# A decoder block on one core: the SSD's output product by pairs of blocks in seven products, with h parked in memory meanwhile

## The chip, the core and the metric

The kernel runs on one core of a Trainium2 chip. A core has TensorE (PE, matrix products into the PSUM banks; its weight loads are listed as PEld), VectorE (DVE), ScalarE (ACT), GpSimd (POOL) and SyncE (SP). SP's queue issues nearly all DMAs here, one after the other in the order of its program. Metric: device time of one execution in microseconds (us), lower is better.

## What is computed

One decoder block on a sequence of 1024 tokens of width 1024, all in float32. The part that matters here:

```python
h = rms_norm(x, pre_norm1_w) * (1.0 + sc1) + sh1
proj = h @ w_in
z, xbc, dt_raw, q, k, v, gates = split(proj)
y_ssd = ssd_branch(z, xbc, dt_raw, ...)             # 1024 x 1024
y_att = diff_attention_branch(q, k, v, ...)         # partial rope on q and k
gate_ssd, gate_att = split(sigmoid(gates))
merged = gate_ssd * (y_ssd @ w_ssd_o) + gate_att * (y_att @ w_attn_o)
mix = merged @ w_out
...                                                 # norms, adaLN gates, conv-FFN
```

The change is about `gate_ssd * (y_ssd @ w_ssd_o)`, which stands between the SSD scan and the attention.

## The kernel before

Every float32 operand of a matmul is split into a high and a low part (type fp32r: ACT copies the high part, DVE subtracts it to get the low one), and a product is three matmuls: high by high, high by low, low by high (`mm3`). A 128 x 512 result over 1024 rows is 8 k-tiles x 3 = 24 matmuls (`block_half`). Activations lie transposed: `hT[k][half]` holds rows 128k of h for 512 tokens, high and low.

Memory on the chip is handed out by `Slots`: 43 slots of 512 KB, first freed, first given again. A tile that gets a freed slot waits for the last use of the tile before it. `hT` holds 16 of the slots from the start of the kernel to the end of the attention.

The order of the work: h; seven-product loops for gates, two q/k blocks and the convolved channels (`pairs`, see below); z; the SSD scan in 16 steps with v's product as filler; then the stage of the change; then attention, with the remaining q/k blocks and the attention's gates as filler (`dense_stream`, `blocks`); its output product; `w_out`; the FFN.

Inside a `with tc.manual_schedule(...)` section the instructions of the engines named there (PE, DVE, ACT and SP for the stages before the attention) run in the order in which the code issues them. Between sections the scheduler may put the first instructions of the next one earlier.

The stage of the change, before:

* Four q/k blocks, `seq` = q0, k0, q1, k1, each for both halves of the tokens. Between the halves TensorE turns the scan's output y (`turn_y`, four transposes per 128 channels and half): ACT scales it into the high part, DVE makes the low part, in `yT[k][half]`. y comes token-wise from memory in four tiles `yr`; `load_y(0)` is issued during the scan, `load_y(1)` after the last turn of the first half.
* `rope` of a finished q/k block: ACT copies it from PSUM, DVE shuffles, POOL and DVE multiply by the tables, DVE adds, `split` makes high and low, and `store_qk` writes them with 16 DMAs of 64 KB. In the loop, `load_y(1)` is called ahead of that `store_qk`:

```python
                if n == 1 and half == 0:
                    load_y(1)
                if half == 0 and old is not None:
                    store_qk(*old[:2], hi, lo)
```

* Eight blocks of `w_ssd_o`, 48 matmuls each; DVE multiplies by (1 + gate) from `gth` (memory `gsd`) and SP writes `msd`. `load_qk(0)` and `load_qk(1)`, which fetch q and k of the first head pair for the attention, are issued at blocks 3 and 4.

The seven-product loop, which exists for gates, q2/k2 and channels: two output blocks (rows of a weight pair) by two halves of tokens, over two halves of the 1024 rows, are a 2 x 2 by 2 x 2 block product. `order` lists the seven products with the bank X, Y or Z that they add to; `HX` holds the right operands (b11, b21, b22 and the sums t1 to t4), `x_sum` and `x_split` make the left ones from the weights, `x_load` fetches these, `x_ahead(m, p)` prepares product p of pair m three products ahead, `x_mms` issues its 12 matmuls. Between the products ACT copies bank X or Y (`ev_`) and DVE adds.

The first attention items: 14 fills of three matmuls each, then `scores(0)`, which needs both tiles that `load_qk` fetched.

Of the kernel before, what the change touches and what calls it, by code (L numbers as in the profile page):

```python
# [62 lines left out]
def kernel(ctx: ExitStack, tc: tile.TileContext, a: dict, out: bass.AP, dbg=None):  # L63
# [306 lines left out]


# [44 lines left out]
    def x_load():  # L416
# [4 lines left out]
        src = {"gs": ("w_gate", "w_gate"), "xbc": ("w_xbc", "w_xbc"), "qk": ("w_q", "w_k")}[kind]["fv".index(n)]  # L421
# [109 lines left out]
    with tc.manual_schedule(engines={EN.PE, EN.DVE, EN.Activation, EN.SP}):  # L531
# [100 lines left out]
        for m, (kind, *_) in enumerate(pairs):  # L632
# [10 lines left out]
            for p in range(7):  # L643
# [161 lines left out]
    def ada_row(r):  # L805
# [7 lines left out]
        if r in (0, 3):  # L813
            ps, row = ps_wb(f"adar{r}"), sm2[:KD, 896 : 896 + P]
            T.transpose(ps[:KD, :P], c_, ident)
            V.tensor_copy(row, ps[:KD, :P])
            SP.dma_start(rowd[r].rearrange("o (k p) -> (o k) p", p=P), row)

    last_pair = len(pairs) - 1
    with tc.manual_schedule(engines={EN.PE, EN.DVE, EN.Activation, EN.SP}):  # L820
        for t_, (c0, wdt) in enumerate(thirds):
# [4 lines left out]
            for i in range(8):  # L826
# [257 lines left out]
    seq = [("w_q", 0), ("w_k", 0), ("w_q", 1), ("w_k", 1)] + [("w_ssd_o", j) for j in range(8)]  # L1084
# [12 lines left out]
    n_skip = 0  # L1097

    def sum_dn(u):
        nonlocal n_skip  # L1100
        if u in (7, 8) and n_skip < 4:
            n_skip += 1
        else:
            next(sums_dn, None)

    with tc.manual_schedule(engines={EN.PE, EN.DVE, EN.Activation, EN.SP}):
# [19 lines left out]
        for u in range(16):  # L1126
# [5 lines left out]
            sum_dn(u)  # L1132
# [3 lines left out]
            sum_dn(u)  # L1136
# [6 lines left out]
            sum_dn(u)  # L1143
# [3 lines left out]
            sum_dn(u)  # L1147
# [26 lines left out]
    yT = [[None] * 2 for _ in range(KD)]  # L1174

    n_turn = 0


    def turn_y(k, half):
        yT[k][half] = new_hl(f"yT{k}_{half}")  # L1180
        nonlocal n_turn
        ps = (ps_wa, ps_wb, ps_wa, ps_wc)[n_turn % 4](f"ytr{k}_{half}")
# [4 lines left out]
        A.activation(yT[k][half][:, 0, :], ps, AF.Copy, scale=nw)  # L1187
        V.scalar_tensor_tensor(yT[k][half][:, 1, :], ps, nw, yT[k][half][:, 0, :].bitcast(F32), op0=ALU.mult, op1=ALU.subtract)
# [4 lines left out]
    perm = [(i + 8) % 16 + 16 * (i // 16) for i in range(32)]  # L1193
    def split_seq(n):
# [6 lines left out]
    def rope(kind, b, ps):  # L1201
        A.activation(qf, ps.rearrange("p h t -> p (h t)"), AF.Copy, scale=qscale[kind])
        V.stream_shuffle(sw, qf, perm)
        G.tensor_tensor(qf, qf, ropc, op=ALU.mult)
        V.tensor_tensor(sw, sw, rops, op=ALU.mult)
        V.tensor_tensor(qf, qf, sw, op=ALU.add)
        split(hi, lo, qf)

    turns = [((0, 1), (2, 3, 4)), ((5, 6, 7), ()), ((0, 1), (2, 3)), ((4, 5), (6, 7))]
    with tc.manual_schedule(engines={EN.PE, EN.DVE, EN.Activation, EN.SP}):  # L1210
        split_seq(0)
        old = None
        for n in range(4):
            fetch_seq(n + 2)
            ps = ps_mm(f"{seq[n][0]}p{seq[n][1]}")
            for half in range(2):
                block_half(ps[:, half, :], seq_w[n], hT, half)
                if half == 0:
                    if old is not None:
                        rope(*old)  # L1220
                    split_seq(n + 1)
                for k in turns[n][half]:
                    turn_y(k, n // 2)
                if n == 1 and half == 0:
                    load_y(1)
                if half == 0 and old is not None:
                    store_qk(*old[:2], hi, lo)
            old = (*seq[n], ps)
        SL.put(*yr)


        gths = [SL.get(f"gth{i}") for i in range(2)]
# [1100 lines left out]
```

## Time and profile before

| | us |
|---|---|
| median of 3 runs | 1862.75 (1860.8 to 1863.04) |
| the profiled execution | 1863.45 |
| its span (first to last instruction) | 1861.5 |
| PE busy | 1827.3 |
| DVE busy | 1290.8 |
| ACT busy | 888.4 |
| POOL busy | 141.6 |

Rows of the profile read: line, engine, operation, output <- input, shapes, count, then busy time or start and length. "idle before <- X" names what ended the wait ahead of an instruction. SPq rows are DMA issues on SP's queue; their length is the time of the issue, not of the transfer. Stretches are given in us from the start of the span.

### The profile page before, as it was taken

The page shows a single profiled execution, that of the slowest core. Times are in us where ns is not written, and L with a number is a line of the kernel's source. Part 1 is how long each engine was busy: PE and PEld are TensorE (multiplying, and loading weights), DVE is VectorE, ACT ScalarE, POOL GpSimd, SP SyncE. Part 2 cuts the span into 40 slices and gives each one's busy share as a digit, 9 for nine tenths or more (in the row PEclk, how much of TensorE's full clock was granted, in tenths as well). Part 3 has the DMA queues.
Part 4 walks back from the last instruction along what each step waited for, and adds up shares of the span by engine and source line. Part 5 has one row for each costly group of instructions (what it writes and reads, how often), then busy time and mean ns, then how long its engine had stood idle before and what let it go on. Part 6 is the DMA issues. An engine that isn't in the chain of part 4 may idle for free.

```text
span 1861.5 us, 24406 instructions
## 1 busy us (share of the span) xinstructions
PE 1827.3 (98%) x8974; PEld 1528.6 (82%) x8974; DVE 1290.8 (69%) x1980; ACT 888.4 (48%) x1720; POOL 141.6 (8%) x128
## 2 busy tenths in 40 slices
PE   6999999999999999999999999999999999999998
PEld 4888889987888888888887888888888888888887
DVE  6777857688755247777767464487898888876545
ACT  6644543455533136565656322564545455455532
POOL 0000000155521000000000000000000000000001
PEclk9999999999999999999999999999999999999999
DMA  8365356587747746656643655123333323378754
GB/s 329 134 215 181 102 190 226 182 313 278 261 128 189 237 136 180 169 162 182 171 130 120 234 195 203 45 91 106 101 116 109 111 86 107 108 229 297 252 159 164
DMA packets 130217, 322.57 MB, mean 173 GB/s; under 512 B 14881, under 2 KB 38833, under 8 KB 130098
## 3 DMA queue, kind: packets, MB, share of 16 engines
q1 hardware_dynamic: 129138, 317.86, 52.6%
q0 software_dynamic: 960, 3.15, 0.5%
q8 instruction: 71, 1.16, 0.3%
q14 instruction: 48, 0.39, 0.1%
HBM read 225.79 MB, written 95.17 MB: 172 GB/s over the span
## 4 chain that ended last, share of the span: by engine, by line
PE 82%; DVE 8%; ACT 4%; DMA 4%; issue 2%; SPq 1%; POOL 0%; DVEq 0%; POOLq 0%; ACTq 0%
PE upx L1741 4%; PE upx L1742 4%; PE upx L1740 4%; PE o L1435 3%; PE upy L1741 2%; PE upy L1740 2%; PE upy L1742 2%; PE dx L2104 2%; PE dx L2105 2%; PE dx L2103 2%; PE dy L2105 2%; PE dy L2103 2%; PE dy L2104 2%; PE at L1422 2%; PE sc L1377 2%
## 5 line engine op out<-in xcount | busy, mean ns | idle before, releaser
L1740 PE MATMUL upx<-t,wu_t 128*128 128x512 f32 x264 | 103.1, 391 | 0.5 <-DVE cv L2168 0.4
L1741 PE MATMUL upx<-t,wu_t 128*128 128x512 f32 x264 | 102.8, 390 | 0.2 <-DVE t L1858 0.2
L1742 PE MATMUL upx<-t,wu_t 128*128 128x512 f32 x264 | 102.7, 389 | 0.0
L1714 ACT ACTIVATE wu_t<-sab 128x512 fp32r<-128x512 f32 x57 | 34.1, 627 | 128.4 <-DVE sab L1731 128.4
L1423 ACT COPY aT<-at 128x512 f32<-128x512 f32 (+2 forms) x96 | 46.1, 480 | 96.0 <-PE at L1422 96.0
L1435 PEld LDWEIGHTS o<-vt,aT 128*128 128x128 f32 x576 | 75.3, 191 | 9.2 <-ACT aT L1423 4.6
L95 DVE TENSOR_TENSOR g_lo<-gst,g_hi 128x1024 fp32r<-128x1024 f32 (+1 forms) x42 | 47.5, 1134 | 50.0 <-ACT g_hi L94 50.0
L1435 PE MATMUL o<-vt,aT 128*128 128x128 f32 x576 | 80.9, 276 | 0.4
L94 ACT ACTIVATE g_hi<-gst 128x1024 fp32r<-128x1024 f32 (+1 forms) x42 | 41.3, 987 | 64.7 <-DMA gst<-gld_s 36.3
L1396 DVE TENSOR_REDUCE nmx<-sc 128x1 f32<-128x640 f32 (+3 forms) x64 | 65.6, 1024 | 2.2
L1376 PE MATMUL sc<-kst,qst 128*128 128x512 f32 (+2 forms) x192 | 63.8, 340 | 0.0
L1377 PE MATMUL sc<-klo,qst 128*128 128x512 f32 (+2 forms) x192 | 63.3, 346 | 0.0
L1758 DVE SCALAR_TENSOR_TENSOR ug<-cg,vec,ug 128x1023 f32<-128x1023 f32 (+1 forms) x44 | 56.3, 1280 | 6.1 <-ACT ug L1757 5.3
L1740 PEld LDWEIGHTS upx<-t,wu_t 128*128 128x128 f32 x264 | 49.6, 188 | 11.6 <-DVE cv L2168 1.3
L1741 PEld LDWEIGHTS upx<-t,wu_t 128*128 128x128 f32 x264 | 49.6, 188 | 10.7 <-DVE t L1858 0.5
L1742 PEld LDWEIGHTS upx<-t,wu_t 128*128 128x128 f32 x264 | 49.6, 188 | 10.2
L1718 DVE TENSOR_TENSOR wu_t<-sab,wu_t 128x512 fp32r<-128x512 f32 x57 | 39.3, 690 | 26.6 <-ACT wu_t L1714 26.6
L1758 DVE SCALAR_TENSOR_TENSOR uv<-cv,vec,uv 128x1023 f32<-128x1023 f32 (+1 forms) x44 | 56.2, 1277 | 0.9 <-ACT uv L1757 0.9
L1414 DVE SCALAR_TENSOR_TENSOR p<-p,coef,p 128x128 f32<-128x128 f32 (+3 forms) x64 | 52.4, 818 | 2.3
L1412 DVE RECIPROCAL rsm<-ssum 128x2 f32<-128x2 f32 x64 | 10.6, 165 | 62.4 <-ACT p L1409 35.2
L2224 POOL TENSOR_TENSOR rsf<-rsf,nhalf 128x1 f32<-128x1 f32 x8 | 5.3, 656 | 624.3 <-DVE rsf L2223 624.3
L2104 PE MATMUL dx<-wdt_lo,g_hi 128*128 128x512 f32 x132 | 51.5, 390 | 0.0
(537 smaller groups left out, 5921.7 us busy)
## 6 DMA issues: line engine op xcount, KB each, us to landing
adas<-in_w_ada SPq DMA_DIRECT2D x32, 512.0 KB, 5.0
wdr<-in_w_down SPq DMA_DIRECT2D x22, 512.0 KB, 5.6
wtd<-wds SPq DMA_DIRECT2D x22, 512.0 KB, 4.0
wuf<-in_w_up SPq DMA_DIRECT2D x22, 512.0 KB, 3.5
gld_s<-gsum SPq DMA_DIRECT2D x22, 512.0 KB, 2.8
gst<-gld_s SPq DMA_DIRECT2D x20, 512.0 KB, 4.6
wdt_raw<-wtd SPq DMA_DIRECT2D x20, 512.0 KB, 5.0
wuv<-in_w_up SPq DMA_DIRECT2D x19, 512.0 KB, 3.5
```

The lines of the kernel that those rows point to most:

```text
L1376: T.matmul(sc[:, n0:n1], qs_[s][:, tsl], ks_[s][:, n0:n1], start=True, stop=False)
L1377: T.matmul(sc[:, n0:n1], qs_[s][:, tsl], kl[s][:, n0:n1], start=False, stop=True)
L1396: V.reduce_max(nmx[:, bq, s : s + 1], sc[:, :L], axis=AX.X, negate=True)
L1414: V.scalar_tensor_tensor(pr[0][:, :L], pr[1][:, :L], coef[:, bq : bq + 1], pr[0][:, :L], op0=ALU.mult, op1=ALU.add)
L1435: T.matmul(po_of[j, grp][:, qi, :], at[:, k, :], vt[j % 2][:, kt, :], start=(kt == 0), stop=(kt == i))
L1740: T.matmul(out_, wh, xh_, start=(k == 0 and first), stop=False, skip_group_check=not first)
L1741: T.matmul(out_, wh, xl_, start=False, stop=False, skip_group_check=not first)
L1742: T.matmul(out_, wl, xh_, start=False, stop=(k == end), skip_group_check=not first)
L1758: V.scalar_tensor_tensor(u[:, d:], c_[:, : S - d], fw[:, 2 - d : 3 - d], u[:, d:], op0=ALU.mult, op1=ALU.add)
L2103: T.matmul(o, gh[:, kk, tsl], wh, start=(k == 0 and not more), stop=False, skip_group_check=more)
L2104: T.matmul(o, gh[:, kk, tsl], wl, start=False, stop=False, skip_group_check=more)
L2105: T.matmul(o, gl[:, kk, tsl], wh, start=False, stop=(k == KF - 1), skip_group_check=more)
```

## The change

The eight blocks of `w_ssd_o` become four pairs of the seven-product loop: 4 x 7 x 12 = 336 matmuls in place of 384. That needs the sums of y's quarters as operands, in float32 and split: `y11, y21, y12, y22`, and `HX` of b11, b21, t2, t1, t3, b22, t4 (28 slots). For these h leaves the chip:

* 12 of the 16 tiles of `hT` are written to memory (`hd`) in the earlier loop of pairs, at pairs 4 to 6; the other four are there already (`h12d`). `h_back` reloads all 16, four at product 5 of the third pair and four at each of the products 0 to 2 of the last.
* The q/k blocks run as (0,0) (0,1) (1,0) (1,1) (2,0) (3,0) (2,1) (3,1), in (block, half), so that the first halves of h are done early. The turns of y's second half come at (1,1), (2,0) and (3,0).
* `rope` becomes a generator of four steps, the last of which calls `store_qk`. For blocks 0 and 1 it runs at once (`rope_now`); for 2 and 3 a step after each product of the new loop.
* `load_qk(0)` and `load_qk(1)` move to products 5 and 6 of the last pair; `fetch(0)` and `fetch(1)`, the first weights of the attention's filler, to its products 0 and 3.

Beside this: the two rows of adaLN that are turned on TensorE are turned two or three z-tiles after their sums (`ada_turn`), sums of adaLN are dealt out differently, the four skipped steps of `sum_dn` lie two in step 7 and two in step 8, and two of the last 20 fills move into the last but one attention item.

```diff
@@ pairs 4 to 6 of the earlier loop
+                if 4 <= m < 7 and p % 2 == 0:
+                    k, half = h_out[4 * (m - 4) + p // 2]
+                    SP.dma_start(hd[k, half], hT[k][half].rearrange("p h t -> p (h t)").bitcast(F32))
-                if p < {1: 7, 2: 5, 3: 2}.get(m, 0):
+                if p < {1: 7, 2: 4, 3: 3}.get(m, 0):
@@ adaLN
-                if nz in (2, 7, 13, 22):
-                    ada_row((2, 7, 13, 22).index(nz))
+                if nz in (2, 7, 13, 21):
+                    ada_row((2, 7, 13, 21).index(nz))
+                elif nz in (5, 23):
+                    ada_turn((5, 23).index(nz) * 3)
...
-                        ada_sum()
+                        for _ in range({6: 0, 14: 0, 10: 2, 18: 2}.get(nz, 1)):
+                            ada_sum()
@@ turns of y
+        if half == 0:
+            n, src = (("b11", y11), ("b21", y21))[c]
+            A.activation(HX[n][kk][:, 0, :], ps, AF.Copy, scale=nw)
+            A.activation(part(src, kk), ps, AF.Copy, scale=nw)
+            lo_of(n, kk, src)
+        elif c == 0:
+            V.scalar_tensor_tensor(part(y12, kk), ps, nw, part(y11, kk), op0=ALU.mult, op1=ALU.subtract)
+        else:
+            A.activation(part(y22, kk), ps, AF.Copy, scale=nw)
@@ rope
+    def rope(n, q_):
+        V.stream_shuffle(sw, q_, perm)
+        yield
+        G.tensor_tensor(q_, q_, ropc, op=ALU.mult)
+        V.tensor_tensor(sw, sw, rops, op=ALU.mult)
+        yield
+        V.tensor_tensor(q_, q_, sw, op=ALU.add)
+        A.activation(hi, q_, AF.Copy)
+        yield
+        V.tensor_tensor(lo, q_, hi.bitcast(F32), op=ALU.subtract)
+        store_qk(*seq[n], hi, lo)
+        yield
+    def rope_now(n):
+        rope_in(n, qf)
+        for _ in rope(n, qf):
+            pass
+    def h_back(n):
+        for _ in range(n):
+            half, k = divmod(n_back[0], KD)
+            n_back[0] += 1
+            hT[k][half] = new_hl(f"hb{k}_{half}")
+            SP.dma_start(hT[k][half].rearrange("p h t -> p (h t)").bitcast(F32), hd[k, half])
@@ the stage
+    turns = {(0, 0): (0, 1), (0, 1): (2, 3, 4), (1, 0): (5, 6, 7), (1, 1): (0, 4), (2, 0): (1, 5, 2), (3, 0): (6, 3, 7)}
+        for n, half in ((0, 0), (0, 1), (1, 0), (1, 1), (2, 0), (3, 0), (2, 1), (3, 1)):
...
+            block_half(ps_of[n][:, half, :], seq_w[n], hT, half)
+            if (n, half) in ((0, 0), (1, 0), (2, 0)):
+                split_seq(n + 1)
+            if half == 0 and n in (1, 2):
+                rope_now(n - 1)
+            for k in turns.get((n, half), ()):
+                turn_y(k, 0 if (n, half) < (1, 1) else 1)
+            if (n, half) == (1, 0):
+                load_y(1)
+            elif (n, half) == (3, 0):
...
+                for k in range(KH):
+                    sub(yt2, y22, y12, k)
+                    hi_of("t2", k, yt2)
+                x_load()
+                for k in range(KH):
+                    lo_of("t2", k, yt2)
+                x_split(m0, 0)
+            elif (n, half) == (2, 1):
+                x_split(m0, 1)
+                for i in range(2):
+                    x_sum(m0, i)
+                for k in range(KH):
+                    hi_of("t1", k, y12)
+                x_split(m0, 2)
+                for k in range(KH):
+                    lo_of("t1", k, y12)
+                for i in range(2, 4):
+                    x_sum(m0, i)
...
+        for m in range(m0, len(pairs)):
...
+            for p in range(7):
...
+                x_mms(m, p)
+                if p == 0:
+                    if m > m0:
+                        out_so(1, first, xbank[m - 1]["X"])
+                        SP.dma_start(msd[j - 1], cgv[1])
+                        x_sum(m, 3)
+                    x_ahead(m, 3)
...
+                elif p == 2:
+                    V.tensor_tensor(cg[:, :HALF], bank["Z"], ev_[:, 0, :], op=ALU.add)
+                    x_ahead(m, 5)
+                    if m == m0:
+                        for k in range(KH):
+                            sub(y21, y21, yt2, k)
...
+                        for k in range(KH):
+                            hi_of("t4", k, y21)
+                elif p == 3:
+                    A.copy(ev_[:, 1, :], bank["X"])
+                    x_ahead(m, 6)
...
+                    for n in range(2):
+                        SP.dma_start(gths[n], gsd[j + n])
...
+                elif p == 5:
+                    V.tensor_tensor(cv[:, HALF:], bank["X"], ev_[:, 0, :], op=ALU.add)
+                    x_sum(m + 1, 0)
+                    x_ahead(m, 8)
+                    out_so(1, second, cv[:, second])
+                else:
+                    V.tensor_tensor(cg[:, HALF:], bank["Y"], ev_[:, 1, :], op=ALU.add)
+                    x_sum(m + 1, 1)
+                    x_ahead(m, 9)
+                    out_so(0, slice(0, S), cg)
+                    SP.dma_start(msd[j], cg)
...
+                if last:
+                    if p == 0:
+                        fetch(0)
+                    elif p == 3:
+                        SL.put(*sab)
+                        fetch(1)
+                    SL.put(*HX[order[p][0]])
+                    if p < 3:
+                        h_back(4)
...
+                    elif p > 4:
+                        load_qk(p - 5, qst[0][p - 5], kst[0][p - 5], klo[0][p - 5])
+                elif m == len(pairs) - 2 and p == 5:
+                    h_back(4)
@@ attention
+            quota += 2 if t == len(items) - 2 else 0
-        for n in range(NLAST):
+        for n in range(NLAST - 2):
```

More of the change, by code (lines that the diff above doesn't have):

```diff
@@ L1096, with sum_dn @@
     sums_dn = all_sums()
[L1097 to L1103, printed above, removed]
+    def sum_dn(u, n):
+        if u not in (7, 8) or n > 1:
             next(sums_dn, None)
@@ L1198, in split_seq, with rope_in @@
             split(*seq_w[n], raw)
[L1201 to L1204, printed above, removed]
[L1205 to L1209 removed]
+    def rope_in(n, dst):
+        A.activation(dst, ps_of[n].rearrange("p h t -> p (h t)"), AF.Copy, scale=qscale[seq[n][0]])
@@ new lines, with fetch @@
+    blocks = [(kind, b) for b in (3, 4, 5) for kind in ("w_q", "w_k")] + [("ga", 0)]
+    blocks += [(kind, b) for b in (6, 7) for kind in ("w_q", "w_k")] + [("ga", g) for g in range(1, 8)]
+    raws, splits = {}, {}
+    def fetch(n):
+        if n < len(blocks):
+            kind, j = blocks[n]
+            raws[n] = wp.tile([P, KD, P], F32, tag="wraw", name=f"{kind}{j}_raw", bufs=3)
+            SP.dma_start(raws[n].rearrange("p k c -> p (k c)"), a["w_gate"][8 + j] if kind == "ga" else a[kind][j])
@@ L1210 @@
+    ps_of = {}
     with tc.manual_schedule(engines={EN.PE, EN.DVE, EN.Activation, EN.SP}):
         split_seq(0)
[L1212 to L1228, printed above, removed]
```

161 lines of the change are left out of this document (108 added, 53 removed).

## The prediction

> **What bounds the kernel now.** I read the page first, then the busy time by stretch, the matmuls of the output product, TensorE's waits, and last the order of the queues around the change.
>
> ```profile
> span 1861.5 us, 24406 instructions
> ...
> PE 1827.3 (98%) x8974; PEld 1528.6 (82%) x8974; DVE 1290.8 (69%) x1980; ACT 888.4 (48%) x1720; POOL 141.6 (8%) x128
> ...
> PE 82%; DVE 8%; ACT 4%; DMA 4%; issue 2%; SPq 1%; POOL 0%; DVEq 0%; POOLq 0%; ACTq 0%
> ```
>
> TensorE (PE) is busy 98% of the span and holds 82% of the chain. So a matmul less is time won, and a wait of TensorE is time lost. The two stretches that the change rewrites, by engine (length, then busy us of PE, PEld, DVE, ACT, POOL; granted clock, DMA share, GB/s):
>
> ```profile
> 523.35:574.20 50.85, 50.85 (x257) 42.77 (x256) 29.60 (x36) 19.34 (x29) 11.36 (x5) 1.00 0.47 124
> 574.20:661.40 87.20, 87.07 (x386) 71.78 (x385) 26.25 (x33) 12.64 (x15) 3.43 (x1) 1.00 0.76 226
> ```
>
> The first is the four q/k blocks with the transposes of y, the second the output product. TensorE has no gap in either; DVE is busy 56 of 138 us. The change gives DVE, ACT and the DMA queue more to do and TensorE less, so the question is whether the cover holds.
>
> **The change part by part.** The matmuls of the product now, with first and last start:
>
> ```profile
> L116 PE MATMUL so<-yT,w_ssd_o_hi x128: 389/389/474, 574.2 to 661.1; 128*128 128x512 f32 x128
> L118 PE MATMUL so<-yT,w_ssd_o_lo x128: 389/389/499, 574.8 to 661.6; 128*128 128x512 f32 x128
> ```
>
> 384 matmuls start within 661.6 - 574.2 = 87.4 us, one every 0.228 us. Four pairs of seven products of 12 are 336; 48 fewer are 48 x 0.228 = **-10.9 us**. A product of 12 lasts 2.73 us. The q/k blocks only change their order (192 matmuls and 64 transposes stay).
>
> ```profile
> PE adar L815 <- DVE mcol L812: 3.0, 1, 3.0
> PE adar L815 <- DVE mcol L810: 0.6, 1, 0.6
> PE pst L1046 <- DVE tt L1029: 1.7, 2, 1.3
> PE xx L462 <- DVE xcv L668: 0.7, 1, 0.7
> ```
>
> The two adaLN rows are now turned two and three tiles after they are summed, so these two waits (3.6 us) should go; as DVE stays as late as it was, I take **-3.0 us** (bounds 0 and -3.6). The shifted skips of `sum_dn` and the two fills moved from the tail change no count; nearest row 1.7 us, so 0 with +-1.7.
>
> The 12 stores of h (6.3 MB) go into the pairs 4 to 6:
>
> ```profile
> 30.00:40.00 10.00, 10.00 (x49) 8.22 (x48) 7.95 (x16) 5.96 (x10) 0.00 (x0) 0.88 1.02 404
> 162.00:220.00 58.00, 58.00 (x258) 48.04 (x257) 45.14 (x60) 29.62 (x45) 0.00 (x0) 1.00 0.40 121
> ```
>
> The second row is about where those pairs run (TensorE 58.00 of 58 us); the first is the fullest stretch of the DMA engines. The stores add 108 GB/s to a share of 0.40, so I cost them at nothing; without that cover each would put a weight load back by its own 1.3 us (0.524 MB at 404 GB/s).
>
> **The second half of y.** Now the SP queue loads it ahead of the first rope's stores, and TensorE asks for it one q/k block later:
>
> ```profile
> 543.37 2.00 SPq L1082 DMA_DIRECT2D yr<-yd  x4
> 546.01 0.32 SPq L387 DMA_DIRECT2D qd<-thhi  x1
> ...
> 552.38 0.30 SPq L388 DMA_DIRECT2D qd<-thlo  x1
> ...
> 558.73 0.30 SPq L390 DMA_DIRECT2D khd<-thhi  x1
> ...
> 567.82 0.42 SPq L1091 DMA_DIRECT2D w_ssd_o_raw<-in_w_ssd_o  x1
> ```
>
> ```profile
> 536.02 1.85 ACT L1187 ACTIVATE yT<-ytr,vec 128x512 fp32r<-128x512 f32 x3 [5.09 <-PE ytr L1185]
> 537.75 1.04 ACT L1202 ACTIVATE qf<-w_qp 128x1024 f32<-128x1024 f32 x1
> ...
> 545.89 1.04 ACT L94 ACTIVATE w_q_hi<-w_q_raw 128x1024 fp32r<-128x1024 f32 x1
> ```
>
> ```profile
> SPq L388 <- DMA yr<-yd: 1.7, 2, 1.1
> ```
>
> ```profile
> 549.00 0.39 PE L116 MATMUL w_qp<-hT,w_q_hi 128*128 128x512 f32 x1
> ```
>
> In the change the rope's last step itself calls `store_qk`, and `rope_now(0)` stands before `load_y(1)`: 16 stores come to stand ahead of the four loads. And `turns[(1, 1)]` asks for the new y already at the end of block (1, 1), which is 549.0 now (the next block starts there). The rope's first store comes 546.01 - 537.75 = 8.3 us after its first ACT copy. In front of that copy ACT gets three more copies of y (1.85 us) and the weight split (1.0): the first store moves from 546.0 to 549. The second group of 16 stores took 567.82 - 558.73 = 9.1 us of SP, so the loads of y are issued at 558 instead of 543.4. The four landed 9.0 us after the first issue (SP's last wait for them ends with its issue at 552.38): 567, or 565 if nothing else moves. TensorE stands from 549.0 to 565-567; I take **+16.5 us**, ends 3.4 (552.4 - 549.0, the loads keeping their place) and 18. Behind the waiting transposes stands all of TensorE's queue; and rope 1 on ACT and DVE, behind the copies of y, starts that much later too.
>
> A long wait has a second price, in the granted clock of the kernel's start (same columns as above):
>
> ```profile
> 26.00:28.00 2.00, 1.83 (x4) 1.01 (x5) 2.00 (x6) 1.83 (x4) 0.00 (x0) 0.50 1.03 401
> ...
> 30.00:32.00 2.00, 2.00 (x9) 1.60 (x8) 1.47 (x3) 0.64 (x1) 0.00 (x0) 0.50 1.03 410
> 32.00:34.00 2.00, 2.00 (x11) 1.62 (x10) 1.16 (x3) 0.81 (x2) 0.00 (x0) 0.90 1.01 404
> ```
>
> After sparse work TensorE ran about 4 us of dense matmuls at 0.50, which is 2 us lost: **+2** for this wait (0 to 4, if the wait at the end has it as well). [...]
>
> **The first pair is short of DVE.** Back to back, a 512-wide DVE operation takes 0.60 us (652.95 - 652.35):
>
> ```profile
> 652.35 0.69 DVE L1301 TENSOR_TENSOR w_q_lo<-w_q_raw,w_q_hi 128x512 fp32r<-128x512 f32 x1
> 652.95 1.29 DVE L1301 TENSOR_TENSOR w_k_lo<-w_k_raw,w_k_hi 128x512 fp32r<-128x512 f32 x2
> ...
> 546.01 1.23 DVE L95 TENSOR_TENSOR thlo<-qf,thhi 128x1024 fp32r<-128x1024 f32 x1 [1.13 <-ACT thhi L94]
> ```
>
> Product 5 of the first pair adds to bank X, which ACT must have copied first; that copy stands on ACT behind the four high parts of t4, these behind DVE. From the last transposes of y until then DVE has 39 operations (12 subtractions, 16 low parts, 6 weight low parts, 4 weight sums, one eviction), 39 x 0.60 = 23.4 us; TensorE has (2, 1), (3, 1) and four products, 96 x 0.228 = 21.9. That is 1.5 us short, with 1.2 for the two ACT operations at the end; the handovers between ACT and DVE cost 1.1 each as in the row, two of them 2; the second weight load stands on SP behind rope 1's 16 stores, about 1.5. So 6 us there. In the second pair the gate loads stand behind rope 2's 16 stores (9.1 us), DVE waits for them at product 6 with the next pair's weight parts behind it: 2 more. **+8 us**, ends 2 and 13. Pairs three and four have steady work; the earlier loop of the same kind had one wait of 0.7 us (the last row of the waits).
>
> **h comes back at the end.** Twelve of the 16 reloads can be issued only when the last pair's first three products free their slots, and the gate loads, the next weights and `load_qk` stand behind them.
>
> ```profile
> kst<-khd SPq DMA_DIRECT2D x4, 256.0 KB, 9.0
> klo<-kld SPq DMA_DIRECT2D x4, 256.0 KB, 9.4
> ```
>
> ```profile
> 661.82 0.39 PE L1330 MATMUL w_qp<-hT,w_q_hi 128*128 128x512 f32 x1
> ...
> 671.34 0.22 PE L1376 MATMUL sc<-kst,qst 128*128 128x128 f32 x1
> ```
>
> Ahead of the last gate tile lie 17 transfers of 512 KB (2 of the product, 1 weight, 12 of h, 2 gates), 8.9 MB; at 404 GB/s 22.1 us from the end of product 1. Six products are 16.4 us, so the gates land about 6 us after the pairs end. Then DVE writes the gated output (five halves, 3 us), SP stores it, and only behind that store issues `load_qk(1)`, whose parts land some 9.2 us later as in the rows: 18.2 us after the pairs. TensorE has 9.5 us of fills before the first scores (671.34 - 661.82). **+9 us**; ends 3 (h comes back early) and 15 (at 300 GB/s). [...]
>
> **The sum.** -10.9 - 3.0 + 16.5 + 2 + 8 + 9 = +21.6. The profiled execution took 1863.45 us (span 1861.5 and 1.95 around it), the median is 0.7 lower: 1863.45 + 21.6 - 0.7 = **1884 us**.
>
> **The rivals.**
> Faster: the loads of y do not stand behind the stores and the rest is covered. It decides at 549.0: y must be there, which means issued by 540, with DVE less than 2 us late and h back before the scores. For it: the count of matmuls is sure, and the earlier loop of pairs runs almost without waits. Against: the order of the calls. -10.9 - 3.0, with 0 to 5 of small waits, is 1849 to 1854.
> Only the wait for y is real; DVE and the reload are covered: -13.9 + 18.5 is 1867. For it: both terms are small differences of long sums.
> Only the DVE and reload terms are real, y waits 3.4: -13.9 + 3.4 + 17 is 1869. For it: SP might hold the stores back less than the rows show.
>
> **How the numbers follow.** All three losses: 0.65, from 1874 (y 15, no clock price, DVE 4, reload 6) to 1894 (18, 3, 11, 13). Only y 0.15, only the other two 0.09, faster 0.11. A measurement of this kernel can tell about 0.2%, 3.7 us. The range 1865 to 1894 holds these three but for some 2 in 10 at their edges and the faster case. Where "only y" comes out at its lower end it lies within 3.7 us of 1862.75, and so would a faster case with 10 us of waits: same 0.06, faster 0.11, slower 0.83.
>
> **What would show it.** In the profile after: a wait of PE at the transposes of y for the DMA of yr of 10 us or more, with `yr<-yd` on SP behind 16 issues of `qd`; 336 matmuls of the product; waits of PE in the first pair behind ACT's copy of bank X; DVE's gated output of the last pair waiting for the gate's DMA, then scores waiting for `kst` and `klo`; a granted clock under 1 after the long wait; no wait at `adar`. I am wrong if `yr<-yd` is issued near 543, or if TensorE is dense from 549 to the first scores.

## The result, and the profile after

The changed kernel takes 1893.72 us (median of 4, 1892.6 to 1896.85) where the kernel before takes 1862.89 beside it: 1.0168 times as long, 95% interval 1.0151 to 1.0186. The forecast was 1884. The profiled executions have spans of 1890.8 and 1861.5 us, 29.3 apart.

The page of the changed kernel, then the three stretches (columns as in the prediction: q/k blocks, output product, from there to the end of the attention's first two scores), each with its counterpart of before:

```profile
span 1890.8 us, 24501 instructions
...
PE 1826.3 (97%) x8926; PEld 1525.7 (81%) x8926; DVE 1336.6 (71%) x2052; ACT 916.2 (48%) x1776; POOL 141.0 (7%) x128
...
PE 84%; DVE 6%; DMA 4%; ACT 3%; issue 1%; SPq 1%; POOL 1%; DVEq 0%; POOLq 0%; ACTq 0%
```

```profile
514.80:583.60 68.80, 54.22 (x257) 44.58 (x256) 30.87 (x41) 26.68 (x43) 7.73 (x4) 0.88 0.35 96
583.60:675.60 92.00, 82.09 (x337) 66.20 (x336) 67.24 (x96) 31.33 (x55) 4.78 (x2) 0.94 0.58 191
675.60:701.50 25.90, 12.52 (x49) 9.67 (x47) 4.92 (x7) 1.63 (x3) 0.00 (x0) 0.79 1.02 329
```

TensorE has 48 matmuls fewer (8974 to 8926) and yet nearly the same busy time (1827.3 to 1826.3): matmuls at a lower granted clock last longer (the 128x512 ones of the product 0.63 us at 0.50 and 0.39 at 1.00). TensorE's clock was 1.00 in all three stretches of before. The two profiles side by side:

| stretch | before | after | difference |
|---|---|---|---|
| up to the q/k blocks | 523.6 | 514.8 | -8.8 |
| q/k blocks | 50.6 | 68.8 | +18.2 |
| output product | 87.6 | 92.0 | +4.4 |
| to the scores | 9.9 | 25.9 | +16.0 |
| all the rest | 1189.8 | 1189.3 | -0.5 |

TensorE's waits in the three stretches (before: 0.13 us idle in them):

```profile
PE ytr L1194 <- DMA yr<-yd: 14.6, 4, 11.7
PE w_qp L1490 <- DVE scg L1394: 6.4, 1, 6.4
PE sx L466 <- ACT yevs L1351: 6.0, 2, 3.7
PE sc L1536 <- DMA kst<-khd: 4.9, 1, 4.9
PE sx L466 <- ACT yevs L1374: 3.1, 1, 3.1
PE sc L1537 <- DMA klo<-kld: 2.1, 2, 1.1
PE sy L466 <- ACT yevs L1386: 0.8, 1, 0.8
```

The waits that the prediction named are there: 14.6 us for y, 9.9 in the product, 13.4 at the end. The order on SP's queue that makes the first:

```profile
547.89 0.42 SPq L392 DMA_DIRECT2D qd<-thlo  x1
548.40 1.80 SPq L1093 DMA_DIRECT2D yr<-yd  x4
```

ACT's operations that hold up its copies of bank X (the copies start at 590.89, 601.30 and 620.49): the high parts of t3 and of t4 in the first pair and the late rope's high part in the second, each waiting for DVE. The waits of TensorE behind these three copies are 2.3, 3.1 and 3.7 us:

```profile
587.97 2.49 ACT L558 ACTIVATE yt<-ys 128x512 fp32r<-128x512 f32 x4 [4.06 <-DVE ys L564]
...
599.02 2.37 ACT L558 ACTIVATE yt<-ys 128x512 fp32r<-128x512 f32 x4 [4.43 <-DVE ys L564]
...
619.52 1.06 ACT L1228 ACTIVATE thhi<-qf 128x1024 fp32r<-128x1024 f32 x1 [4.31 <-DVE qf L1227]
```

And the lines of DVE behind which the waits at the end stand:

```profile
686.29 0.69 DVE L1324 SCALAR_TENSOR_TENSOR scv<-gth,scv 128x512 f32<-128x512 f32 x1 [15.11 <-DMA gth<-gsd]
686.90 0.68 DVE L1394 TENSOR_TENSOR scg<-sy,yevs 128x512 f32<-128x512 f32 x1
```

### The profile page after: what moved, and what is told of

It is laid out like the page before. It is cut to its first block, busy times and chain, and to the rows that moved or that the text cites. A ratio compares the mean times of both kernels' runs of the same rounds, so it can differ in the third digit from the quotient of the medians.

```text
span 1890.8 us, 24501 instructions
## 1 busy us (share of the span) xinstructions
PE 1826.3 (97%) x8926; PEld 1525.7 (81%) x8926; DVE 1336.6 (71%) x2052; ACT 916.2 (48%) x1776; POOL 141.0 (7%) x128
## 4 chain that ended last, share of the span: by engine, by line
PE 84%; DVE 6%; DMA 4%; ACT 3%; issue 1%; SPq 1%; POOL 1%; DVEq 0%; POOLq 0%; ACTq 0%
PE upx L1902 4%; PE upx L1903 4%; PE upx L1901 4%; PE o L1595 3%; PE dx L2265 2%; PE dx L2266 2%; PE dx L2264 2%; PE upy L1903 2%; PE upy L1902 2%; PE upy L1901 2%; PE z L117 2%; PE z L118 2%; PE z L116 2%; PE dy L2266 2%; PE dy L2264 2%; PE dy L2265 2%
## 5 line engine op out<-in xcount | busy, mean ns | idle before, releaser
L1490 PE MATMUL gap<-hb,ga_hi 128*128 128x512 f32 x128 | 56.5, 441 | 0.0
L1572 DVE RECIPROCAL rsm<-ssum 128x2 f32<-128x2 f32 x64 | 10.6, 165 | 62.4 <-ACT p L1569 35.1
```

What stands on the lines that cost most here:

```text
L1490: T.matmul(ps, w[0][:, k, :], xh_, start=(k == 0), stop=False)
```

## The experiments

All are compared by their medians with 1893.72 (after) and 1862.5 to 1862.9 (before, measured beside each).

**The side edits alone**, in the kernel before:

```diff
-                if nz in (2, 7, 13, 22):
-                    ada_row((2, 7, 13, 22).index(nz))
+                if nz in (2, 7, 13, 21):
+                    ada_row((2, 7, 13, 21).index(nz))
+                elif nz in (5, 23):
+                    ada_turn((5, 23).index(nz) * 3)
...
-            sum_dn(u)
+            sum_dn(u, 0)
```

> The kernel before with the side edits alone (the two adaLN rows turned later, the sums dealt anew, the shifted skips of sum_dn, the two fills moved); the output product and the q/k blocks stay as before. Theory A, a wait of TensorE costs its length and then some matmuls at a halved clock: the stretch up to the q/k blocks ends 7 to 9 us earlier, as in the changed kernel (514.8 for 523.6), so 1854 to 1856. Rival, the waits count with their length alone: the two waits of 3.6 us go, 1859 to 1860. Rival, the 8.8 us come from elsewhere in the change (the stores of h, the pairs): 1862 to 1863.

Measured: 1853.1 us, 0.9947 times before (0.9932 to 0.9962). The waits of TensorE in z and v, 3.0 + 0.9 + 0.6 us before, are gone, and z takes 92.3 us for 100.3. The q/k blocks begin at 515.0, where the changed kernel has 514.8, so the stores of h, which this kernel does not have, cost nothing that shows. What one of these waits does in the kernel before, in 2 us windows from 262 on (the wait of 3.01 us ends at 266.7):

```profile
264.00:266.00 2.00, 0.00 (x0) 0.00 (x0) 1.53 (x2) 0.44 (x1) 0.00 (x0) 1.00 1.06 364
266.00:268.00 2.00, 1.30 (x9) 1.30 (x10) 0.85 (x5) 0.00 (x0) 0.00 (x0) 0.98 0.69 270
268.00:270.00 2.00, 2.00 (x9) 2.00 (x8) 0.00 (x0) 0.00 (x0) 0.00 (x0) 0.50 0.60 156
270.00:272.00 2.00, 2.00 (x11) 2.00 (x9) 0.00 (x0) 0.00 (x0) 0.00 (x0) 0.67 0.29 117
272.00:274.00 2.00, 2.00 (x14) 2.00 (x14) 1.07 (x3) 1.38 (x2) 0.00 (x0) 1.00 0.00 0
```

The clock falls to 0.50 only after the matmuls have resumed: 20 in the 4 us from 268 on, where 14 run in the next 2. The side edits are worth three times what was forecast, and this kernel is faster than both.

**The price of one long wait**, in the kernel before (loads of y behind the first rope's stores, two turns of y half a block earlier):

```diff
-                if n == 1 and half == 0:
-                    load_y(1)
...
+                    store_qk(*old[:2], hi, lo)
+                    load_y(1)
...
-    turns = [((0, 1), (2, 3, 4)), ((5, 6, 7), ()), ((0, 1), (2, 3)), ((4, 5), (6, 7))]
+    turns = [((0, 1), (2, 3, 4)), ((5, 6, 7), (0, 1)), ((), (2, 3)), ((4, 5), (6, 7))]
```

> The kernel before with one change: the four loads of the second half of y stand behind the first rope's 16 stores on SP, and the first two of its transposes come one half block earlier, as in the changed kernel. One long wait of TensorE in a stretch that is dense otherwise, so the time over the wait's own length is the price in granted clock. Theory A (from the changed kernel's q/k stretch, 18.2 us for a wait of 14.6): a wait of 12 to 15 us and 3 to 4 us more, 1878 to 1881. The prediction's step: the same wait and 2 us, 1876 to 1879. Rival, no price, the stretch was longer for another reason: the wait alone, and a granted clock of 1.00 behind it.

Measured: 1877.0 us, 1.0080 times before (1.0063 to 1.0096). One wait, and the clock behind it:

```profile
PE ytr L1185 <- DMA yr<-yd: 12.1, 4, 9.0
```

```profile
560.00:562.00 2.00, 1.02 (x4) 0.73 (x5) 0.00 (x0) 0.03 (x1) 0.00 (x0) 0.50 0.58 238
562.00:564.00 2.00, 2.00 (x8) 1.71 (x7) 1.21 (x2) 1.83 (x3) 0.00 (x0) 0.50 0.01 2
564.00:566.00 2.00, 2.00 (x7) 1.52 (x5) 1.80 (x4) 0.43 (x1) 0.16 (x1) 0.50 0.00 0
566.00:568.00 2.00, 2.00 (x10) 1.67 (x9) 1.02 (x1) 0.00 (x0) 2.00 (x1) 0.99 0.00 0
```

The q/k blocks take 66.2 us (522.4 to 588.6) for 50.6: 12.1 of wait and 3.5 of clock. By the times alone (+14.2 us) the price is 2, with an interval too wide to tell 2 from 3.5; the trace tells it.

**The loads of y ahead of the rope**, in the changed kernel:

```diff
-            if half == 0 and n in (1, 2):
-                rope_now(n - 1)
+            if (n, half) == (2, 0):
+                rope_now(1)
...
                 load_y(1)
+                rope_now(0)
```

> The changed kernel with the loads of the second half of y called ahead of the first rope, so that they stand before its 16 stores on SP; nothing else. Theory A (16 stores ahead of the loads made the wait, and the wait cost clock besides): the loads are issued near 541, the wait at the transposes falls from 14.6 us to 2 to 5, the q/k stretch from 68.8 us to 54 to 57, the time from 1893.7 to 1879 to 1882. Rival, the wait alone counts and the clock is low in that stretch for another reason: 1883 to 1885. Rival, the order on SP was not the cause (the loads take long or y is stored late): the wait stays over 10 us, 1890 to 1894.

Measured: 1884.3 us. The loads go out at 534.45, and the wait is 4.6 us in another form: 2.1 for y and 2.5 for DVE, which evicts a turn only behind the second rope, whose high part waits until the first rope's stores have read the tile. The q/k stretch is 57.6 us. So the order on SP made the wait, but the ropes held the turns as well. With the turns ahead of both ropes and none after block (1, 1):

```diff
-    turns = {..., (1, 1): (0, 4), (2, 0): (1, 5, 2), (3, 0): (6, 3, 7)}
+    turns = {..., (2, 0): (0, 4, 1, 5, 2), (3, 0): (6, 3, 7)}
...
             if (n, half) == (1, 0):
                 load_y(1)
+            if half == 0 and n in (1, 2):
+                rope_now(n - 1)
```

> The changed kernel with both calls of load_y and the new transposes ahead of the rope's steps in every q/k block, and the first new transposes after block (2, 0): neither SP's stores nor the rope's waits on DVE stand ahead of y. Theory A (the wait at the transposes is an order of queues alone): the wait falls from 14.6 us to 0 to 2, the q/k stretch to 51 to 54 us, the time to 1876 to 1880. Rival, y's second half makes DVE and ACT late in any order and the wait is handed on into the product: 1881 to 1888.

Measured: 1886.2 us, the rival. The wait at the transposes is 1.3 us and the q/k stretch 52.3 us at a clock of 1.00, 16.5 less; but the product waits 15.6 us instead of 9.9. DVE and SP show why:

```profile
PE sx L466 <- ACT yevs L1351: 12.6, 2, 8.0
```

```profile
571.82 0.69 DVE L450 TENSOR_TENSOR ysab<-xwv 128x512 f32<-128x512 f32 x1 [4.75 <-DMA xwv<-in_w_ssd_o]
```

```profile
556.55 0.42 SPq L427 DMA_DIRECT2D xwf<-in_w_ssd_o  x1
559.15 0.30 SPq L394 DMA_DIRECT2D khd<-thhi  x1
...
566.79 0.42 SPq L395 DMA_DIRECT2D kld<-thlo  x1
567.25 0.42 SPq L427 DMA_DIRECT2D xwv<-in_w_ssd_o  x1
```

The product's second weight tile, xwv, stands behind the second rope's 16 stores, as y stood behind the first's. In the changed kernel the wait for y hid most of it (DVE waited 1.68 us there).

**That load one q/k block earlier**, on top of the last:

```diff
-                else:
-                    x_load()
+                elif n == 2:
+                    x_load()
+                    x_load()
```

> The run with y in order (1886.2, product waits 15.6 us) with one call moved: the second weight load of the output product (xwv) is called one q/k block earlier, ahead of the second rope's 16 stores on SP. Theory A (DVE stood 4.75 us behind that load, and ACT's copies behind DVE): DVE no longer waits for xwv, the first pair's waits fall from 10.6 us to 4 to 6, 1879 to 1883. Rival, DVE has too much to do there whenever the weights land: 1885 to 1887.

Measured: 1878.9 us. The first pair's waits are 3.2 + 4.7, more than expected, for 8.0 + 1.8 + 0.4 (the 10.6 in the text above takes in one of the third pair); the product's stretch falls from 97.9 to 93.4.

**ACT's copies.** A first attempt in the changed kernel itself put the high parts of t3 and t4 behind ACT's copies of bank X and a rope's step one product later:

```diff
-            hi_of("t3", k, y11)
...
                     A.copy(ev_[:, 1, :], bank["X"])
...
+                            hi_of("t4", k, y21)
                             lo_of("t4", k, y21)
...
-                while ropes and (m, p) != (m0, 6):
+                while ropes and (m, p) not in ((m0, 6), (m0 + 1, 0)):
```

> The changed kernel with three steps put behind ACT's copies of bank X: the high parts of t3 behind the first copy of the first pair, those of t4 behind the second, and the second rope's addition and high part one product later; no instruction more or less. Theory A (the copies stood in ACT's queue behind operations that wait for DVE, though their own input was ready): the waits behind the copies (6.0 and 3.1 us) go and some 4 us of clock with them, 1880 to 1884. Rival, DVE is short of time in the first pairs in any order: the same time is waited for at the operands of t3, t4 or the weight parts, 1890 to 1894.

Measured: 1896.7 us, the rival: 11.3 us of waits, 4.1 of them now for the copy of bank Y, which had come to stand behind t4. On top of the run with y and xwv in order, with t4 behind the copy of Y too and one of the first pair's gate loads a product later, it is another matter:

```diff
                     A.copy(ev_[:, 0, :], bank["Y"])
...
+                            hi_of("t4", k, y21)
+                            lo_of("t4", k, y21)
...
-                while ropes and (m, p) != (m0, 6):
+                while ropes and (m, p) != (m0 + 1, 3):
```

> As the run with xwv moved, and ACT's queue in another order: the high parts of t3 behind the first copy of bank X, those of t4 behind the copy of bank Y, the second late rope one product later where it stood ahead of a copy. Theory A (what is left are copies behind operations that wait for DVE): the product's waits fall to 2 to 5 us, its stretch from 92.0 us to 79 to 83, the time to 1870 to 1876. Rival, DVE is short by itself: the waits move to the operands of t3, b22 and t4, 1879 to 1884, as in the first run that moved these copies.

Measured: 1874.7 us; waits 9.0, stretch 90.5: between the two theories. The four times go from 1873.5 to 1881.9, so the 4.2 us between this run and the last are known only to a few us; the product's stretch is 2.9 us shorter. The product's longest wait, 4.8 us, is for DVE's eviction of bank X, and behind it DVE has no gap left (columns as above; third pair of numbers is DVE):

```profile
566.00:576.00 10.00, 10.00 (x46) 8.29 (x45) 9.30 (x17) 7.62 (x13) 0.00 (x0) 1.00 0.33 104
576.00:586.00 10.00, 7.27 (x31) 5.18 (x29) 10.00 (x18) 5.69 (x11) 0.00 (x0) 1.00 0.13 39
586.00:596.00 10.00, 7.41 (x23) 5.94 (x24) 9.30 (x13) 1.67 (x3) 2.36 (x1) 0.66 0.31 120
```

**DVE's load.** Eight subtractions on GpSimd, in the changed kernel:

```diff
-            sub(y11, yt2, y11, k)
+            G.tensor_tensor(part(y11, k), part(yt2, k), part(y11, k), op=ALU.subtract)
...
-                            sub(y21, y21, yt2, k)
+                            G.tensor_tensor(part(y21, k), part(y21, k), part(yt2, k), op=ALU.subtract)
```

> The changed kernel with the eight subtractions that make t3 and t4 on GpSimd instead of DVE, at the same places; nothing else. Theory A (DVE is short in the first pair, and ACT's copies wait behind what waits for DVE): 4.8 us less of DVE ahead of the second copy; the waits of the product fall from 9.9 us to 3 to 6, the time from 1893.7 to 1885 to 1889. Rival, the waits come from ACT's and SP's order alone: no change, 1892 to 1895. Rival, GpSimd's operations are so slow or slow DVE so much that t3 or t4 is late: slower, over 1895.

Measured: 1894.0 us, no change. The relief was eaten: while GpSimd worked, from 571.6 to 585.2, four of DVE's low parts took 6.89 us, and after it 2.49 (a row's second number is the time of all its instructions):

```profile
575.44 6.89 DVE L561 TENSOR_TENSOR yt<-yt,yt 128x512 fp32r<-128x512 f32 x4
...
588.32 2.49 DVE L561 TENSOR_TENSOR yt<-ys,yt 128x512 fp32r<-128x512 f32 x4
```

The other way is to take the work out, first in the changed kernel, then with all queues in order:

```diff
-                    lo_of("t2", k, yt2)
...
-                    lo_of("t1", k, y12)
...
-                            lo_of("t3", k, y11)
...
-                            lo_of("b22", k, y22)
```

> The changed kernel without the 16 low parts of t2, t1, t3 and b22 (the product reads their high parts twice, so its numbers are less exact): 16 x 0.60 = 9.6 us less of DVE ahead of the second copy, nothing handed to another engine. Theory A (DVE is short between the last transposes and the second pair): the product's waits fall from 9.9 us to 0 to 3 and their clock goes with them, 1880 to 1885. Rival, the order of ACT and the late weight load on SP make the waits: 1889 to 1893.

Measured: 1888.2 us, next to the rival's 1889: 7.3 of 9.9 us of waits stay.

> The run with all of the product's queues in order (1874.7, product waits 9.0 us), without the 16 low parts of t2, t1, t3 and b22 (high parts read twice): 9.6 us less of DVE. Theory A (what is left is DVE's load in the first pair): the wait of 4.8 us for the eviction of bank X goes and most of the rest, waits 0 to 3 us, stretch 77 to 81 us, 1862 to 1867. Rival, the chains of ropes, sums and evictions keep their length whatever DVE has to do: 1870 to 1874.

Measured: 1871.0 us, 3.7 less than with them (1874.7), by the rival's number; but the wait of 4.8 us for the eviction is 1.0, and the stretch is 85.7 for 90.5. What stays are above all 5.1 us for copies of bank X in the second and third pair.

**The end.** First the order alone, in the changed kernel:

```diff
+                        for n in range(2):
+                            SP.dma_start(gths[n], gsd[j + n])
                         fetch(0)
...
-                        h_back(4)
+                        h_back((4, 4, 1)[p])
...
+                        for s in range(2):
+                            load_qk(s, qst[0][s], kst[0][s], klo[0][s])
...
+                elif m == len(pairs) - 2:
+                    h_back(1)
```

> The changed kernel with its end in another order: seven tiles of h are loaded back during the third pair into the slots that the ropes left free, the last pair's gate loads stand at its first product, and both calls of load_qk at its fourth, ahead of the stores of the gated output; the same bytes. Theory A (the order of the loads made the waits of 6.4 and 7.0 us, with some 2.5 us of clock): the stretch from the last pair to the scores falls from 25.9 us to 10 to 13, the time to 1878 to 1881. Rival, the DMA engines are full there (404 GB/s) and the loads are late in any order: half of it stays, 1885 to 1889. Rival, the earlier loads of h hold back the third pair's weights and gates: a new wait of 2 to 5 us there.

Measured: 1895.1 us. The wait behind the gates is gone and the same time stands at kst and klo:

```profile
PE sc L1539 <- DMA kst<-khd: 10.9, 2, 7.1
PE sc L1540 <- DMA klo<-kld: 2.6, 2, 1.8
```

```profile
686.00:688.00 2.00, 1.11 (x5) 0.57 (x4) 0.00 (x0) 0.00 (x0) 0.00 (x0) 1.00 1.02 406
688.00:690.00 2.00, 0.00 (x0) 0.00 (x0) 0.00 (x0) 0.57 (x2) 0.00 (x0) 1.00 1.08 217
```

The DMA engines are full in both rows (share 1.02 and 1.08), but with h and the weights they move 406 GB/s and with kst and klo 217. Then fewer bytes in the old order, and fewer bytes in the new one:

```diff
+            if half == 1:
+                hT[k][1] = hT[k][0]
+                continue
```

> The changed kernel without the reload of the second half of h (8 of the 16 loads, 4.2 MB less; the attention's blocks read the first half twice, so their numbers are other ones); order and slots as they were. Theory A (at the end the DMA engines are full, and the bytes of h ahead of the gates and of kst and klo make the waits): 4.2 MB at 404 GB/s are 10.4 us, so the waits of 6.4 and 7.0 us fall to 0 to 4 together, the stretch from 25.9 us to 10 to 14, the time to 1878 to 1883. Rival, the order (gates behind h, load_qk behind the store) keeps its waits: 1888 to 1893.

> The run without the reload of h's second half (1884.6), in the order of the run that changed the end's order: last gates ahead, load_qk at the last pair's fourth product. Theory A (bytes and order both count: with all of h the DMA engines are full and the order is idle, without half of it load_qk's place behind the store of the gated output is what is left, 5.3 us of waits): the waits for kst and klo fall to 0 to 1, 1877 to 1880. Rival, the loads of kst and klo are slow in themselves (they ran at 213 to 246 GB/s) and bound the end in any order: 1883 to 1886.

Measured: 1884.6 and 1884.7 us. Half of h is worth 9.1 us and this order, by the time, nothing. What is left at the end in the old order are kst and klo (in the new one 2.8 and 0.9, the product in turn 0.9 us longer):

```profile
PE sc L1540 <- DMA kst<-khd: 4.0, 1, 4.0
PE sc L1541 <- DMA klo<-kld: 1.3, 1, 1.3
```

So these were loaded in the third pair, with y, xwv and ACT's copies in order as above:

```diff
+                elif m == len(pairs) - 2:
...
+                    if p in (0, 4):
+                        load_qk(p // 4, qst[0][p // 4], kst[0][p // 4], klo[0][p // 4])
```

> As the run before it, and at the end q and k of the first two head pairs are loaded in the third pair, into the slots that the ropes left free; all of h but one tile comes in the last pair, the last gates ahead of it. Theory A (the DMA engines are full in the last pair, and q and k are 2.1 MB at half the rate, 9.3 us, that fit into the third pair): the waits at the end fall from 13 us to 1 to 4, the time to 1852 to 1860. Rival, the third pair's gates and weights wait behind them: a new wait there of 3 us or more, 1862 to 1868.

Measured: 1870.5 us, 4.2 less than without it and above the ranges of both theories. The waits at the end are 4.1 us for 11.9, and the product's are 14.1 for 9.0: most of the gain is given back in the third and fourth pair, whose gates and weights now stand behind q and k.

**Sums.** Mends together: first y's loads ahead of the rope, the GpSimd subtractions, the late ropes earlier, and the end's order with h in the second and third pair; then two versions with what could not be mended left out, made of the edits shown above:

> The changed kernel with all mends together: the loads of y ahead of the first rope and its first new transposes half a block later; the subtractions for t3 and t4 on GpSimd; the two late ropes one step earlier and without the skipped step; seven loads of h from the middle of the second pair on, the last gates ahead of the other nine, load_qk at the last pair's fourth product. If the losses add up as measured (y and its clock 18, product up to 15, end up to 16) and each mend takes two thirds, 1859 to 1864. If DVE or the DMA engines only hand the wait on, as in the two runs that changed an order alone, 1872 to 1880. Under 1853 only if no wait is left.

```diff
-                while ropes and (m, p) != (m0, 6):
+                while ropes:
...
+                elif (m0 + 1, 4) <= (m, p) < (m0 + 2, 4):
+                    h_back(1)
```

Measured: 1891.8 us, far over every range. TensorE waited 10.5 us at the turns of y for DVE (five turns behind the second rope), and four of DVE's low parts took 6.88 us beside GpSimd, as in the run with GpSimd's subtractions alone.

> The three runs of this call in one kernel: y in order, 16 low parts left out, half of h's reload left out and the end in order. It tells whether the losses named so far are all there are. Theory A: nothing is left but the 48 matmuls less and the side edits, 1862.8 - 10.9 - 9.4 = 1842.5, and up to 6 us of waits that are left over: 1842 to 1849. Rival, the seven products cost something that no wait shows (the stores of h, the clock, contention): 1850 to 1860.

Measured: 1868.4 us, over both ranges; xwv was late, and the product's waits were 11.6 us.

> The run with the end's loads moved (1870.5) without the 16 low parts and without the reload of h's second half. Theory A (the losses named are all there are): 1862.7 - 9.4 for the side edits - 10.9 for 48 matmuls = 1842.4, and 2 to 8 us of waits left over: 1844 to 1850. Rival, something else costs (contention of the DMA engines with the loads of weights, the clock in dense stretches): 1853 to 1862.

Measured: 1860.2 us, 0.9989 times before (0.9979 to 0.9998). The end is covered now (10.8 us to the first scores), but the product still takes 92.6 us with 11.3 of waits, in the second to the fourth pair, where DVE stands in its order behind late loads:

```profile
614.07 0.69 DVE L1324 SCALAR_TENSOR_TENSOR scv<-gth,scv 128x512 f32<-128x512 f32 x1 [4.64 <-DMA gth<-gsd]
...
637.87 0.69 DVE L450 TENSOR_TENSOR ysab<-xwv 128x512 f32<-128x512 f32 x1 [7.38 <-DMA xwv<-in_w_ssd_o]
```

By the number it is the rival, but the trace shows no cost without a wait or a lower clock; the waits move on and are larger than theory A allowed. The product's stretch, with its clock (columns as above):

```profile
566.80:659.50 92.70, 81.28 (x338) 64.73 (x337) 61.58 (x84) 30.78 (x55) 4.78 (x2) 0.96 0.68 206
```

Theory A's 1842.4, with 13.5 us of waits (1.3 at y, 11.3 in the product, 0.9 at the end) and 3.7 of clock (0.04 of 92.7), is 1859.6; measured are 1860.2. Whether an order exists in which all four pairs run dense was not found.

## Why the prediction was right or wrong

The direction came out, and each of the waits that were named is there, though not each for the reason given; the sum was +21.6 and the spans show +29.3. Term by term, from the two traces (336 matmuls are counted, their price is the prediction's 0.228 us; the clock is the remainder of the three stretches):

| term | forecast | measured |
|---|---|---|
| 48 matmuls | -10.9 | -10.9 |
| adaLN and other side edits | -3.0 | -8.8 |
| wait for y | +16.5 | +14.6 |
| waits in the product | +8 | +9.9 |
| waits at the end | +9 | +13.4 |
| clock behind the waits | +2 | +11.6 |
| all the rest | 0 | -0.5 |

The clock is what a stretch is longer by than its waits and its matmuls account for: 18.2 - 14.6 = 3.6, 4.4 + 10.9 - 9.9 = 5.4 and 16.0 - 13.4 = 2.6, 11.6 together. In the product the granted clock itself shows 5.1 of the 5.4: behind the waits of 2.3, 3.1 and 3.7 us TensorE is busy for 3.4 us each at half the clock, 1.7 us lost each time:

```profile
591.64:595.05 3.41, 3.41 (x9) 2.67 (x10) 3.41 (x7) 2.95 (x6) 0.00 (x0) 0.50 0.00 0
601.88:605.29 3.41, 3.37 (x8) 2.69 (x9) 2.86 (x5) 2.96 (x5) 0.00 (x0) 0.50 0.31 100
622.37:625.78 3.41, 3.41 (x10) 2.64 (x9) 3.41 (x5) 0.20 (x1) 0.00 (x0) 0.50 0.58 147
```

**The step that failed first is "+2 for this wait (0 to 4, if the wait at the end has it as well)".** The price was within its bounds for one wait, 2 forecast and 3.5 shown by the kernel with that wait alone; but it was counted once, with nothing for the waits in the product. In the changed kernel each of the three stretches pays. The long one costs 3.6 us there and 3.5 in the kernel with that wait alone, as its transposes between the waits for y's four tiles run at the halved clock too (0.50 from 548 to 560 in the changed kernel); waits of 2.3 and 3.1 us cost 1.7 us each as well.

**The adaLN term** counted the two waits at the turns and no clock. The waits that went are 4.5 us with those of `wz_lo`, and behind the wait of 3.0 the clock was halved for about 3.4 us (267.9 to 271.3 in the kernel before; 8 or 9 matmuls late, 0.16 us each). That is some 6 of the 8.0 us by which z is shorter; the rest stays open. This error of 5.8 us has the other sign and brought the forecast nearer by luck; without it the forecast would have been off by 13.5.

**The wait for y** came as written: 16 stores ahead of four loads. The whole stage began 8.8 us earlier, and the first store stood at 540.26 instead of 549, so the loads were issued at 548.4 instead of 558 and the wait was asked for earlier as well.

**The product's +8** was near in size and wrong in its parts. "The second weight load stands on SP behind rope 1's 16 stores, about 1.5" was the largest of them: moving that load gave 7.3 us once y was in order. ACT's order gave 4.2 more, DVE's load 3.7. In the changed kernel the late y hid the late weights. The prediction put the first pair's loss at the second copy of bank X alone, which cost 3.1 us; the first copy, behind t3's high parts, cost 2.3 more. In the second pair it put 2 us on the gates. TensorE waited 3.7 us there, but for the copy behind the late rope's high part; DVE did wait 2.5 us for the gates, up to 636.78, and TensorE's next wait is 0.8 us, 14 us later.

**The end's +9** used 9.5 us of fills as cover. Some 4 us of this cover weren't there: the second half of the first q/k block needs the PSUM bank that the last pair's Y holds, and its eviction (scg, at 686.90 above) stands on DVE behind the gated output, which waits for the gates. And the gates landed 10.6 us after the pairs, not 6. The place behind the store, on which the prediction's chain of issues rests, is not the cause alone: the same bytes with kst and klo ahead of that store wait as long. With the DMA engines full (share 1.02 in that stretch), the bytes that the last pair has to load are the cause (half of h was worth 9.1 us), and for q and k the rate (217 GB/s for 406). Moving q and k into the third pair took 7.8 us off the waits at the end, and the product waited 5.1 us more.

**The rival "faster"** named the right condition, y in time and DVE and h covered. The runs that meet it piece by piece go from 1893.7 over 1886.2, 1878.9 and 1874.7 to 1870.5 us, and stay behind the kernel before. None meets it whole: 18.2 us of waits in the product and at the end are left in the last.

## What to carry to other kernels

When TensorE is busy 98% of the time, a transformation that saves matmuls can be paid in the queues around it: before making it, list for each in-order queue what will stand ahead of the next thing that TensorE needs, and price each long wait with some 2 us of clock on top (none to 3.6 behind the waits of 2.3 to 14.6 us in these runs). Mending one wait shows the next one: here y's late load hid a late weight load, and that hid ACT's order and DVE's load, so a term shows its worth only when the waits in front of it are gone. Try the side edits of a change by themselves: here two transposes put behind other work, with some dealing of sums, gave 9.4 us, while the 10.9 us of the new product never reached the end of the kernel, and the version to keep is the old product with the side edits (1853.1 us).

## What the runs showed of the hardware

DVE was slower while GpSimd worked. Four of its 128x512 low parts took 6.89 us beside GpSimd's subtractions (6.88 in the run with all mends together), 1.72 each. The same four in the changed kernel, where GpSimd is idle from 565.4 to 607.5, took 2.49, 0.62 each:

```profile
575.54 2.49 DVE L561 TENSOR_TENSOR yt<-yt,yt 128x512 fp32r<-128x512 f32 x4
```

What in the two engines makes the difference no run tried.

Loads of kst and klo, which go into 64 partitions at a time, moved 217 GB/s with the DMA engines full (share 1.08), and h and the weights, into 128 partitions, 406 (share 1.02). The kernel before shows nearly the same rate, behind the issues of its first `load_qk` (611.12 to 613.55; columns as above):

```profile
616.00:620.00 4.00, 4.00 (x19) 3.30 (x19) 1.50 (x3) 0.00 (x0) 0.00 (x0) 1.00 1.01 215
```

No run tried why these loads are slower.

The clock fell late in places, and behind short waits too. In the last kernel a wait of 2.33 us was followed by full-speed matmuls for 1.5 us and then by half-speed ones for 3 us, while one of 3.24 us had no such sequel (the number after the start is a matmul's duration):

```profile
595.93 0.50 PE L466 MATMUL sx<-yt,xw_t 128*128 128x512 f32 x1 [3.24 <-ACT yevs L1348]
596.27 0.40 PE L467 MATMUL sx<-yt,xw_t 128*128 128x512 f32 x1
...
644.11 0.50 PE L466 MATMUL sx<-yt,xw_t 128*128 128x512 f32 x1 [2.33 <-ACT yevs L1348]
...
645.65 0.63 PE L466 MATMUL sx<-yt,xw_t 128*128 128x512 f32 x1
...
649.01 0.39 PE L468 MATMUL sy<-yt,xw_t 128*128 128x512 f32 x1
```
